# Moving the next pair's keys and queries ahead of the third gate tile in the attention stage of a hybrid encoder layer

## The chip, the cores and the metric

One NeuronCore of a Trainium2 chip runs the whole layer. The metric is device time in microseconds (us). Engines are named as in the profile: PE is TensorE (PEld its weight loads), DVE is VectorE, ACT is ScalarE, POOL is GpSimd and SP is SyncE, which here only issues DMAs.

## The reference, cut to what matters

The layer normalizes x (1024 rows, 1024 columns), projects it, runs three token mixers side by side (a short gated convolution, a strictly causal stick-breaking attention with 16 heads of 64, a cross-attention into 256 memory rows), gates and sums them, and ends with an MLP of width 4096. What this case turns on:

```
proj = rms_norm(x, g_mix) @ w_in       # conv_h|conv_B|conv_C|sb_q|sb_k|sb_v|x_q|gate_pre
for each head, each block of 128 queries:
    z = q @ k.T * 64**-0.5             # keys up to the end of the block
    log_1mb = where(past, log_sigmoid(-z), 0)
    between = reversed cumsum(log_1mb) - log_1mb
    a = where(past, exp(log_sigmoid(z) + between), 0)
    o = a @ v
gates = sigmoid(gate_pre)              # three gates of 1024 columns
x = x + (g0*y_conv + g1*y_sb + g2*y_x) @ w_out
```

## The kernel before

All matrices are float32, and each product is made of three passes with a high and a low half (`mm3`, `mm3_steps`): high by high, high by low, low by high. A weight tile of 128 columns is loaded by SP into one of four buffers (`raw`), then ACT casts the high half (L89) and DVE subtracts it from the raw value (L90) into one of three buffers (`whl`). Everything else lives in a pool of 40 pages (`pg`, 128 x 1024 float32 each), 16 of which hold the transposed and normalized x (`hT`).

The stage of the heads (L666 to L721) runs the stick-breaking attention, two heads (a pair) at a time, eight pairs. A pair has 16 steps: for each head `hd`, eight query blocks `i`. A step calls `sb_weights` (scores z on PE, L553 and L554; two sigmoids on ACT, L555 and L556; two causal masks on POOL, L558; a reversed running product on DVE, L568; a product on DVE, L572). Two steps later `sb_transpose` turns the weights on PE (L582), and ACT (L113) and DVE (L114) split them into halves; a step after that, for every second block, `sb_values` multiplies by the values on PE (L597), with the sum finished on ACT (L606), DVE (L607) and POOL (L608). Transposed blocks go through two PSUM buffers (`t`), filler projections through three (`d`).

Between these dependent pieces the loop puts independent projections, the fillers (L205 to L207). For pair p they are `gate_steps(0, p)`, `gate_steps(1, p)`, `gate_steps(2, p)`, each a column tile of one gate in 4 cuts of 12 matmuls, and `sb_qk(p+1)`: the keys (4 cuts) and then the queries (4 cuts) that the next pair needs. They are chained and handed out by a quota (`goal`, L708), 20 cuts over the 16 steps: 10 for the first head and 10 for the second. The last pair has `conv_steps(0)` in place of `sb_qk`.

What follows a projection's last matmul (`done`) is written down when the next cut is asked for. For a gate it is one sigmoid on ACT per half (L619) and, at the end, a store to DRAM issued by POOL (L621). For keys and queries it is two casts on ACT (L507, L508 or L521, L522) and two subtractions on DVE (L509, L510 or L523, L524) per half; after the keys, SP issues four DMAs that copy 64 rows to the other 64 rows (L514), and they wait for those casts and subtractions.

From L382 on nothing pins the program order (`pin[0] = False`): the order of each engine's queue is settled when the kernel is built, mostly as written, with pieces pulled ahead where something was not ready by the planner's own estimate. At run time each engine takes its queue in order.

Of the kernel before, what the change touches and what calls it, by code (L numbers as in the profile page):

```python
# [36 lines left out]
def f32v(ap):  # L37

    return ap.bitcast(F32)
# [3 lines left out]
def block_kernel(ctx, tc, x, mem, small, w_in, w_v, w_kv, w_co, w_so, w_xo, w_out, w_up, w_dn, out):  # L43
# [19 lines left out]
    def page(dt=F32R, shape=(P, 1024)):  # L63
        return pgp.tile(list(shape), dt, tag="pg", name=nm("pg"))
# [41 lines left out]
    def unit(src, paged=False):  # L106

        return halves(load(src), paged)
# [74 lines left out]
    def run(gen):  # L183
        for _ in gen:
            pass

    def chain(*gens):
        for g in gens:
            yield from g

    def fill(gen, n):
        for _ in range(n):
            next(gen, None)
# [17 lines left out]
    def project_steps(w, th, done, cuts=2):  # L211

        ps = pd()
        yield from mm3_steps(
            ps, [(cut(w, k * P, (k + 1) * P), cut(hT[k], th * 512, th * 512 + 512)) for k in range(KT)], cuts
        )
        done(ps)
# [280 lines left out]
    def sb_qk(p, st):  # L498


        ka, kb, la, lb = page(), page(), page(), page()
        w = unit(w_in[CT_K + p])
        for th in range(2):
            s = slice(th * 512, th * 512 + 512)

            def done(ps):
                nc.scalar.copy(ka[A, s], ps[A])  # L507
                nc.scalar.copy(kb[B, s], ps[B])  # L508
                nc.vector.tensor_tensor(out=la[A, s], in0=ps[A], in1=f32v(ka[A, s]), op=ALU.subtract)  # L509
                nc.vector.tensor_tensor(out=lb[B, s], in0=ps[B], in1=f32v(kb[B, s]), op=ALU.subtract)  # L510

            yield from project_steps(w, th, done)
        for t_, to, from_ in ((ka, B, A), (kb, A, B), (la, B, A), (lb, A, B)):
            nc.sync.dma_start(out=f32v(t_[to]), in_=f32v(t_[from_]))  # L514
        qa, qb = page(), page()
        w = unit(w_in[CT_Q + p])
        for th in range(2):
            s = slice(th * 512, th * 512 + 512)

            def done(ps):  # L520
                nc.scalar.copy(qa[A, s], ps[A])  # L521
                nc.scalar.copy(qb[B, s], ps[B])  # L522
                nc.vector.tensor_tensor(out=qa[B, s], in0=ps[A], in1=f32v(qa[A, s]), op=ALU.subtract)  # L523
                nc.vector.tensor_tensor(out=qb[A, s], in0=ps[B], in1=f32v(qb[B, s]), op=ALU.subtract)  # L524

            yield from project_steps(w, th, done)
        st.update(q=(qa, qb), k=(ka, kb), kl=(la, lb))

    def sb_v(p):

        raw = load(v_scr[p // 4][:, p % 4, :])
        v = []
        for jh in range(2):
            vt = page(F32R, (P, 4, 2, P))
            to = vt.rearrange("p j h e -> p (j h) e")
            src = raw[:, jh * 512 : jh * 512 + 512].rearrange("p (a e) -> p a e", a=8)
            split(src, to[:, :, 0:64], to[:, :, 64:128])
            v.append(vt)
        return v
# [3 lines left out]
    def sb_weights(st, hd, i):  # L543

        q, kh, kl = st["q"][hd], st["k"][hd], st["kl"][hd]
        W = (i + 1) * P
        be, eo = page(F32), page(F32)
        ts_ = slice(i * P, (i + 1) * P)
        for c in range(1 + (i >= 4)):
            w = W if i < 4 else W // 2  # L550
            cs = slice(w * c, w * c + w)
            z = pz()
            nc.tensor.matmul(z[:, 0:w], lhsT=q[:, ts_], rhs=kh[:, cs], start=True, stop=False)  # L553
            nc.tensor.matmul(z[:, 0:w], lhsT=q[:, ts_], rhs=kl[:, cs], start=False, stop=True)  # L554
            nc.scalar.activation(eo[:, cs], z[:, 0:w], AF.Sigmoid, scale=-0.125)  # L555
            nc.scalar.activation(be[:, cs], z[:, 0:w], AF.Sigmoid, scale=0.125)  # L556
        for t_, fill_ in ((eo, 1.0), (be, 0.0)):
            nc.gpsimd.affine_select(  # L558
                out=t_[:, W - P : W],
                in_=t_[:, W - P : W],  # L560
                pattern=[[-1, P]],
                compare_op=ALU.is_gt,
                fill=fill_,
                base=0,
                channel_multiplier=1,
            )
        rev = eo[:, W - 1 :: -1]
        nc.vector.tensor_tensor_scan(  # L568
            out=rev, data0=rev, data1=zero.broadcast_to([P, W]), initial=1.0, op0=ALU.mult, op1=ALU.add
        )  # L570

        nc.vector.tensor_tensor(out=be[:, 0 : W - 1], in0=be[:, 0 : W - 1], in1=eo[:, 1:W], op=ALU.mult)  # L572
        return be
# [38 lines left out]
    def gate_steps(b, d):  # L612
        w = unit(w_in[CT_G + 8 * b + d])
        g = page(F32)
        for th in range(2):
            yield from project_steps(
                w,
                th,
                lambda ps: nc.scalar.activation(g[:, th * 512 : th * 512 + 512], ps, AF.Sigmoid),  # L619
            )  # L620
        nc.gpsimd.dma_start(out=g_scr[b][d], in_=g)  # L621
# [3 lines left out]
    def conv_steps(c):  # L625

        prod = page(F32)
        ch = page(F32)
        w = unit(w_in[CT_H + c])
        for th in range(2):  # L630
            s = slice(th * 512, th * 512 + 512)
            yield from project_steps(w, th, lambda ps: nc.scalar.copy(ch[:, s], ps))
        w = unit(w_in[CT_C + c])
        for th in range(2):
            s = slice(th * 512, th * 512 + 512)
            yield from project_steps(
                w, th, lambda ps: nc.vector.tensor_tensor(out=prod[:, s], in0=ps, in1=ch[:, s], op=ALU.mult)
            )
        cv = page(F32)

        def tap(j):
            return sm[:, C_CONV + 3 * c + j : C_CONV + 3 * c + j + 1]

        nc.scalar.activation(cv, prod, AF.Copy, scale=tap(2))
        for j in (1, 2):
            nc.vector.scalar_tensor_tensor(
                out=cv[:, j:1024],
                in0=prod[:, 0 : 1024 - j],
                scalar=tap(2 - j),
                in1=cv[:, j:1024],  # L650
                op0=ALU.mult,
                op1=ALU.add,
            )
        w = unit(w_in[CT_B + c])
        hl = (page(), page())
        for th in range(2):
            s = slice(th * 512, th * 512 + 512)

            def done(ps):
                nc.vector.tensor_tensor(out=cv[:, s], in0=ps, in1=cv[:, s], op=ALU.mult)  # L660
                split(cv[:, s], hl[0][:, s], hl[1][:, s])

            yield from project_steps(w, th, done)
        u.append(hl)

    nxt = {}  # L666
# [9 lines left out]
    for p in range(NPAIR):  # L676
        st, nxt = nxt, {}
        st.update(p=p)
        gens = [gate_steps(b, p) for b in range(3)]
        nfill = 12  # L680
        if p + 1 < NPAIR:
            gens.append(sb_qk(p + 1, nxt))
            nfill += 8
        else:
            gens.append(conv_steps(0))
            nfill += 9
        more = chain(*gens)
        weight = [i + 4 for i in range(8)]
        total, seen, used = 2 * sum(weight), 0, 0
        for hd in range(2):  # L690
            aT = {}
            for i in range(8):
                be = sb_weights(st, hd, i)
                if hd == 0 and i == 0:
                    st["v"] = sb_v(p)

                def tail_t(st=st, hd=hd, i=i, be=be, aT=aT):
                    if "o" not in st:
                        st["o"] = page(F32)
                    if i % 2 == 0:  # L700
                        aT[i // 2] = [page(F32R, (P, 2, 2, 256)) for _ in range(i // 2 + 1)]
                    sb_transpose(be, i, aT[i // 2])

                todo.append((step[0] + 2, tail_t))
                if i % 2:
                    todo.append((step[0] + 3, lambda st=st, hd=hd, g=i // 2, aT=aT: sb_values(st, hd, g, aT.pop(g))))
                seen += weight[i]
                goal = nfill * seen // total  # L708
                half = (goal - used + 1) // 2
                fill(more, half)  # L710
                todo.sort(key=lambda e: e[0])
                flush(0)
                fill(more, goal - used - half)
                used = goal
                step[0] += 1
        if p + 1 < NPAIR:
            run(more)
# [175 lines left out]
```

## Time and profile before

| | |
|---|---|
| median of 3 runs | 2309.98 us (2309.84 to 2311.8) |
| the profiled execution | 2309.64 us, of which 2307.9 us are the profiled span |
| granted TensorE clock | 1.0 over the whole span |
| busy share of DVE, ACT, POOL | 49%, 35%, 13% |
| the stage of the heads | 332.6 to 1023.1 us of the span |
| starts of pairs 1 to 7 (first z, i = 0, of the first head) | 410.17, 495.61, 581.04, 666.47, 751.90, 837.38, 922.87 us |

A pair takes 85.43 us, and from the second pair on its timeline repeats to within some hundredths of a microsecond, so one pair can be read for all. In the timeline rows below, the columns are the start, the length, the engine, the line with operation and shape, how many neighbours are merged (x), and in brackets the idle time of the engine before it with what ended that. Matmuls overlap, so the distance from one start to the next is what one costs, not its length.

### The profile page before, as it was taken

The numbers are of one execution on the slowest core, as the hardware profiler recorded it, in microseconds if no ns is written. First come the engines' busy times: TensorE is split into PE (matmuls) and PEld (weight loads), VectorE is DVE, ScalarE is ACT, GpSimd is POOL, SyncE is SP. The second block draws the span as 40 slices with busy tenths as digits, with TensorE's granted clock in tenths as the row PEclk, the third lists the DMA queues.
The fourth block names the chain that finished last, engine by engine and source line by source line (L and its number), as shares of the span: only waits on it lengthen the run. The fifth ranks groups of instructions, "written<-read, shape, count | busy, mean of one in ns | idle before, by whom it ended". The sixth has DMA issues, their size and how long they took to land.

```text
span 2307.9 us, 26972 instructions
## 1 busy us (share of the span) xinstructions
PE 2261.2 (98%) x10688; PEld 1880.7 (81%) x10688; DVE 1130.1 (49%) x1589; ACT 803.3 (35%) x1550; POOL 303.3 (13%) x422
## 2 busy tenths in 40 slices
PE   7999999999999999999999999999999999999999
PEld 6988888778778778788888888888888888888887
DVE  5534127787777777763333344443333333333333
ACT  6544235565556555541122121223221221221221
POOL 1021113333334333320000000000000000000000
PEclk9999999999999999999999999999999999999999
DMA  6311322222122122211111443250111111111111
GB/s 220 101 60 68 125 69 76 72 75 81 64 83 73 65 90 65 83 40 52 46 47 63 146 156 128 92 191 1 37 55 55 37 55 52 40 55 48 44 46 73
DMA packets 49455, 174.79 MB, mean 76 GB/s; under 512 B 6065, under 2 KB 6065, under 8 KB 49329
## 3 DMA queue, kind: packets, MB, share of 16 engines
q1 hardware_dynamic: 42160, 147.90, 20.4%
q0 software_dynamic: 7168, 25.17, 2.9%
q8 instruction: 84, 1.38, 0.2%
q14 instruction: 43, 0.34, 0.0%
HBM read 135.29 MB, written 29.36 MB: 71 GB/s over the span
## 4 chain that ended last, share of the span: by engine, by line
PE 82%; DVE 6%; issue 5%; POOL 4%; ACT 3%; DMA 1%; SPq 0%; POOLq 0%; ACTq 0%; DVEq 0%
PE d L205 16%; PE d L207 16%; PE d L206 16%; PE d L125 9%; PE d L127 9%; PE d L126 9%; POOL pg L558 3%; PE o L597 2%; DVE pg L114 1%; PE t L582 1%; DVE pg L572 1%; ACT pg L555 1%; PE z L554 1%; PE z L553 1%; DVE pg L568 1%
## 5 line engine op out<-in xcount | busy, mean ns | idle before, releaser
L205 PE MATMUL d<-pg,whl 128*128 128x512 f32 x1664 | 655.2, 394 | 0.0
L207 PE MATMUL d<-pg,whl 128*128 128x512 f32 x1664 | 649.8, 391 | 0.0
L206 PE MATMUL d<-pg,whl 128*128 128x512 f32 x1664 | 649.4, 390 | 0.0
L207 PEld LDWEIGHTS d<-pg,whl 128*128 128x128 f32 x1664 | 312.4, 188 | 66.5
L206 PEld LDWEIGHTS d<-pg,whl 128*128 128x128 f32 x1664 | 312.7, 188 | 60.1
L205 PEld LDWEIGHTS d<-pg,whl 128*128 128x128 f32 x1664 | 312.7, 188 | 60.1
L90 DVE TENSOR_TENSOR whl<-raw,whl 128x1024 fp32r<-128x1024 f32 x160 | 201.9, 1262 | 302.3 <-ACT whl L89 301.8
L89 ACT CAST whl<-raw 128x1024 fp32r<-128x1024 f32 x160 | 168.6, 1054 | 518.4 <-PE d L127 291.5
L558 POOL TENSOR_SCALAR_AFFINE_SELECT pg<-pg 128x128 f32<-128x128 f32 x256 | 181.2, 713 | 317.4 <-ACT pg L555 301.6
L568 DVE TENSOR_TENSOR_SCAN pg<-pg,zero 128x128 f32<-128x128 f32 (+7 forms) x128 | 176.2, 1377 | 64.3 <-POOL pg L558 62.6
L127 PE MATMUL d<-whl,pg 128*128 128x512 f32 x512 | 199.2, 389 | 0.0
L125 PE MATMUL d<-whl,pg 128*128 128x512 f32 x512 | 199.2, 389 | 0.0
L126 PE MATMUL d<-whl,pg 128*128 128x512 f32 x512 | 199.2, 389 | 0.0
L113 ACT CAST pg<-t 128x256 fp32r<-128x256 f32 (+2 forms) x336 | 115.2, 364 | 212.4 <-DVE pg L114 144.7
L833 DVE TENSOR_TENSOR pg<-d,pg 128x512 f32<-128x512 f32 x128 | 88.3, 690 | 188.8 <-PE d L127 188.5
L114 DVE TENSOR_TENSOR pg<-t,pg 128x256 fp32r<-128x256 f32 (+2 forms) x336 | 129.4, 404 | 69.6 <-ACT pg L113 66.2
L126 PE MATMUL d<-pg,whl 128*128 128x512 f32 x384 | 149.4, 389 | 0.0
L125 PE MATMUL d<-pg,whl 128*128 128x512 f32 x384 | 149.4, 389 | 0.0
L127 PE MATMUL d<-pg,whl 128*128 128x512 f32 x384 | 149.4, 389 | 0.0
L205 PE MATMUL d<-pg,pg 128*128 128x512 f32 (+1 forms) x384 | 138.1, 360 | 1.3 <-ACT pg L116 1.3
L206 PE MATMUL d<-pg,pg 128*128 128x512 f32 (+1 forms) x384 | 136.9, 357 | 0.5 <-DVE pg L90 0.5
L207 PE MATMUL d<-pg,pg 128*128 128x512 f32 (+1 forms) x384 | 136.9, 357 | 0.0
(114 smaller groups left out, 2747.3 us busy)
## 6 DMA issues: line engine op xcount, KB each, us to landing
raw<-in_w_in SPq DMA_DIRECT2D x72, 512.0 KB, 3.6
raw<-in_w_up SPq DMA_DIRECT2D x32, 512.0 KB, 3.7
raw<-in_w_dn SPq DMA_DIRECT2D x32, 512.0 KB, 4.3
gscr<-pg POOLq DMA_DIRECT2D x24, 512.0 KB, 2.9
raw<-gscr SPq DMA_DIRECT2D x24, 512.0 KB, 3.3
raw<-in_w_kv SPq DMA_DIRECT2D x16, 512.0 KB, 4.4
pg<-in_x SPq DMA_DIRECT2D x16, 512.0 KB, 8.2
pg<-pg SPq DMA_DIRECT2D x32, 256.0 KB, 3.4
```

What stands on the lines that cost most here:

```text
L89: a = nc.scalar.copy(hl[0], raw)
L90: b = nc.vector.tensor_tensor(out=hl[1], in0=raw, in1=f32v(hl[0]), op=ALU.subtract)
L113: nc.scalar.copy(hi, src)
L114: nc.vector.tensor_tensor(out=lo, in0=src, in1=f32v(hi), op=ALU.subtract)
L125: nc.tensor.matmul(ps, lhsT=ah, rhs=bh, start=i == 0, stop=False)
L126: nc.tensor.matmul(ps, lhsT=ah, rhs=bl, start=False, stop=False)
L127: nc.tensor.matmul(ps, lhsT=al, rhs=bh, start=False, stop=i == n - 1)
L205: nc.tensor.matmul(ps, lhsT=ah, rhs=bh, start=i == 0, stop=False)
L206: nc.tensor.matmul(ps, lhsT=ah, rhs=bl, start=False, stop=False)
L207: nc.tensor.matmul(ps, lhsT=al, rhs=bh, start=False, stop=i == n - 1)
L558: nc.gpsimd.affine_select(out=t_[:, W - P : W], in_=t_[:, W - P : W], pattern=[[-1, P]], compare_op=ALU.is_gt, fill=fill_, base=0, channel ...
L568: nc.vector.tensor_tensor_scan(out=rev, data0=rev, data1=zero.broadcast_to([P, W]), initial=1.0, op0=ALU.mult, op1=ALU.add)
```

## The change

In the list of the fillers of a pair, `sb_qk(p + 1)` stands third, ahead of the third gate tile, and no longer last. The quota and the number of cuts are the same. The last pair's list is as before.

```
         gens = [gate_steps(b, p) for b in range(3)]
         nfill = 12
         if p + 1 < NPAIR:
-            gens.append(sb_qk(p + 1, nxt))
+            gens.insert(2, sb_qk(p + 1, nxt))
             nfill += 8
         else:
             gens.append(conv_steps(0))
```

## Rows read from the trace of the kernel before

**Rows 1.** The page, busy time of PE: us, share of the span, instructions.
```profile
PE 2261.2 (98%) x10688; PEld 1880.7 (81%) x10688; DVE 1130.1 (49%) x1589; ACT 803.3 (35%) x1550; POOL 303.3 (13%) x422
```
**Rows 2.** Busy us by engine in two stretches: length, PE, PEld, DVE, ACT, POOL.
```profile
581.00:666.40 85.40, 81.54 (x400) 67.12 (x400) 66.39 (x95) 50.18 (x117) 31.93 (x44) 1.00 0.23 74
1038.60:1096.30 57.70, 57.70 (x256) 47.80 (x255) 19.20 (x21) 11.31 (x14) 0.00 (x0) 1.00 0.17 52
```
**Rows 3.** Line L523: durations in ns (min/median/max), and who waited for it (us, times).
```profile
L523 DVE TENSOR_TENSOR pg<-d,pg x16: 683/684/685, 328.6 to 925.5; 64x512 fp32r<-64x512 f32 x16
...
  PE z L553: 7.4, 7
```
**Rows 4.** Timeline of PE where pair 4 starts.
```profile
665.05 0.39 PE L207 MATMUL d<-pg,whl 128*128 128x512 f32 x1
666.47 0.33 PE L553 MATMUL z<-pg,pg 128*128 128x128 f32 x1 [1.04 <-DVE pg L523]
...
667.65 1.95 PE L597 MATMUL o<-pg,pg 128*128 128x512 f32 x6 [0.74 <-DVE pg L114]
...
675.51 0.63 PE L582 MATMUL t<-ident,pg 128*128 128x128 f32 x4 [0.64 <-DVE pg L114]
...
679.47 1.19 PE L597 MATMUL o<-pg,pg 128*128 128x512 f32 x4 [0.78 <-DVE pg L114]
```
**Rows 5.** Timeline of PE where the second head of pair 3 starts.
```profile
624.09 0.39 PE L207 MATMUL d<-pg,whl 128*128 128x512 f32 x1
...
625.12 1.94 PE L597 MATMUL o<-pg,pg 128*128 128x512 f32 x6 [0.46 <-DVE pg L114]
...
634.61 1.87 PE L597 MATMUL o<-pg,pg 128*128 128x512 f32 x8
```
**Rows 6.** Timeline of DVE where pair 4 starts.
```profile
664.48 1.23 DVE L572 TENSOR_TENSOR pg<-pg,pg 128x1023 f32<-128x1023 f32 x1
665.73 0.68 DVE L523 TENSOR_TENSOR pg<-d,pg 64x512 fp32r<-64x512 f32 x1
666.45 0.69 DVE L524 TENSOR_TENSOR pg<-d,pg 64x512 fp32r<-64x512 f32 x1
667.17 1.29 DVE L114 TENSOR_TENSOR pg<-t,pg 128x256 fp32r<-128x256 f32 x3
669.11 0.69 DVE L523 TENSOR_TENSOR pg<-d,pg 64x512 fp32r<-64x512 f32 x1 [0.65 <-ACT pg L522]
...
670.53 0.42 DVE L568 TENSOR_TENSOR_SCAN pg<-pg,zero 128x128 f32<-128x128 f32 x1
```
**Rows 7.** Timeline of ACT where pair 4 starts.
```profile
667.63 0.37 ACT L113 CAST pg<-t 128x256 fp32r<-128x256 f32 x1 [3.84 <-DVE pg L114]
667.90 0.58 ACT L521 CAST pg<-d 64x512 fp32r<-64x512 f32 x1
...
669.10 0.28 ACT L555 ACTIVATE pg<-z 128x128 f32<-128x128 f32 x1
```
**Rows 8.** Timeline of DVE in the first steps of pair 3's second head.
```profile
632.17 0.75 DVE L114 TENSOR_TENSOR pg<-t,pg 128x256 fp32r<-128x256 f32 x2
...
633.82 0.73 DVE L114 TENSOR_TENSOR pg<-t,pg 128x256 fp32r<-128x256 f32 x2
...
636.38 1.23 DVE L90 TENSOR_TENSOR whl<-raw,whl 128x1024 fp32r<-128x1024 f32 x1 [1.36 <-ACT whl L89]
```
**Rows 9.** Timeline of ACT there: the third gate's first sigmoid.
```profile
630.71 0.62 ACT L619 ACTIVATE pg<-d 128x512 f32<-128x512 f32 x1
```
**Rows 10.** Line L621: the gates' stores issued by POOL (ns, min/median/max).
```profile
L621 POOL DMA_DIRECT2D gscr<-pg x24: 548/571/582, 347.0 to 975.2; - x24
```
**Rows 11.** Timeline of POOL where pair 4 starts.
```profile
669.44 0.54 POOL L558 TENSOR_SCALAR_AFFINE_SELECT pg<-pg 128x128 f32<-128x128 f32 x2 [5.00 <-ACT pg L555]
```
**Rows 12.** Timeline of SP in pair 3: the row copies, and the weight load behind them.
```profile
650.97 3.12 SPq L514 DMA_DIRECT2D pg<-pg  x4
658.33 0.33 SPq L83 DMA_DIRECT2D raw<-in_w_in  x1
```

More of the change, by code (lines that the diff above doesn't have):

```diff
@@ L681, in block_kernel @@
         if p + 1 < NPAIR:
-            gens.append(sb_qk(p + 1, nxt))
+            gens.insert(2, sb_qk(p + 1, nxt))
             nfill += 8
```

## The prediction

> **What bounds the kernel now.** I read the page's busy times first, then the busy times by stretch, then who waited for the queries' subtraction, and last the timelines of PE, DVE and ACT around the start of a pair. PE is busy for 2261.2 of 2307.9 us [rows 1], so PE sets the time, and only its idle time can be won by a new order of the same matmuls. Outside this stage there is next to none: in a stretch of the convolutions PE is busy for 57.70 of 57.70 us [rows 2]. In pair 3 it is busy for 81.54 of 85.40 us [rows 2], so a pair holds 3.86 us of idle PE, and seven pairs that start on queries prepared in the loop hold 27 us. That is all that can be at stake for a gain.
>
> Where in a pair it lies is read from PE's timeline. At the start of pair 4 PE idles 1.04 us before the first z, until DVE has subtracted the queries, then 0.74 us before the values (L597), then 0.64 us before a transpose and 0.78 us before the next values, the last three for a split on DVE [rows 4]: 3.20 us in the first 14 us of a pair. At the start of the second head, where the same steps run without new queries, there is one gap of 0.46 us [rows 5]. The queries' wait is found for all seven pairs: 7 times, 7.4 us [rows 3].
>
> **The change part by part.** No instruction is added or removed. The filler cuts have fixed places in the loop, and 20 of them stay 20; weight splits come every fourth cut for whichever tile is next. What moves is what follows the matmuls. Count the cuts of a pair from 0: before, cuts 8 to 11 are the third gate, 12 to 15 keys, 16 to 19 queries; after, 8 to 11 keys, 12 to 15 queries, 16 to 19 the third gate. The follow-up of a half is written with the cut after it. So at cuts 14 and 16, queries stand where keys stood, with equal work (two casts, two subtractions). At cut 18 and at the pair's end, two sigmoids stand where the queries' casts and subtractions were; at cuts 10 and 12, in the first steps of the second head, keys stand where sigmoids were. In sum two halves' work moves from the end of the pair to the start of its second head: for each half, two subtractions of 0.68 and 0.69 us [rows 6] on DVE and, on ACT, two casts of 0.58 us [rows 7] in place of one sigmoid of 0.62 us [rows 9].
>
> *Term A, the pair's start.* Before, DVE ends the last product (L572) at 665.71, then does the first half's two subtractions, and only at 667.17 the splits that the values wait for [rows 6]; the values start at 667.65, 2.60 us after the last filler matmul at 665.05 [rows 4]. After, the queries have been ready since cut 16, so z follows the filler at once, and with the two subtractions out of the queue the splits move up behind L572, to 665.73. That is 667.17 - 665.73 = 1.44 us, and the values start at about 666.21, 1.16 us after the last filler. The row that stands nearest agrees: at the second head that distance is 625.12 - 624.09 = 1.03 us [rows 5]. What is late next is thus the same split, so not all of 1.04 + 0.74 us goes. Bounds: nothing, if the splits don't move up, and 2.60 - 1.03 = 1.57 us. I take 1.44.
>
> *Term B, the two gaps after it.* Behind the values come the second half's casts and subtractions: DVE is held by them from 669.11 to about 670.50, with 0.65 us of idle before [rows 6], because ACT does its casts first, 667.90 to 669.07, and only then the sigmoid of z, 669.10 [rows 7]. After, ACT has one sigmoid there: 1.16 - 0.62 = 0.54 us less, on top of the 1.44, so z's sigmoid, its mask and the scan (L568, before at 670.53) come 1.98 us earlier; if the scan follows DVE's own queue, it is 1.44 + 1.39 = 2.83 us less what POOL's queue gives back (below), about 2.4. All that follows on DVE moves up by 2.0 to 2.4 us, PE by 1.44 alone: the splits gain 0.56 to 0.96 us on PE, and the gaps of 0.64 and 0.78 us [rows 4] shrink by so much. Bounds: nothing and 1.42. I take the middle, 0.75.
>
> *Term C, the second head.* Here the keys' work is new, and DVE has less room than its 49% say. Before, the four splits of the last block run at 632.17 (two) and 633.82 (two, to 634.55) [rows 8], and the eight values that need them start at 634.61 without a gap [rows 5]: just in time. The keys' first half takes its place at ACT's sigmoid of 630.71 [rows 9], and its 1.38 us on DVE stand ahead of the splits, which then run at about 633.6 and 635.2 to 635.95. The values' first four need only the first two splits; the fifth, (1.87 - 0.39) / 7 = 0.21 us apart, is due at 635.46 and gets its split at about 635.6. So PE loses about 0.15 us. The second half (cut 12) falls next to DVE's idle 1.36 us before L90 [rows 8], which covers it. If that cover is gone, and both halves reach PE in full, C is 2 x 1.38 = 2.76 us. Lower bound 0. I take 0.15, by the due times of the rows, which are the nearest of all.
>
> *The queues.* SP's four row copies now wait for keys that are done four cuts sooner; behind them stands a weight load that before went out at 658.33, 4.3 us after the copies ended [rows 12], so it hangs on a free buffer and not on them: nothing. POOL's store of the third gate moves from the second head's fourth step to the pair's end, ahead of the first masks. POOL is held there for its wait and 0.57 us [rows 10], and the masks, which before came after 5.00 us of idle [rows 11], would start 0.6 us later than they could: this is in B's lower value. The subtractions themselves cost the same anywhere, 683 to 685 ns in 16 cases [rows 3].
>
> *Pages.* Counted from the code in program order, from first write to last read, the stage needs at most 36 of 40 pages before and 38 after, because keys and queries are held longer. The Trainium skill (Perfetto Trace Analysis, Optimization Strategy) says that the same gap repeating on the engine that should be saturated can mean that there is not enough buffer space for the next tile. The gaps here do repeat every 85.43 us, yet the rows name a subtraction and splits as what ended them, so I don't follow it; by it the change, which holds more pages, would give nothing back and lose time, and that is the third rival.
>
> **The sum.** A + B - C = 1.44 + 0.75 - 0.15 = 2.04 us a pair. Seven pairs have B and A at their start, and seven have C: 7 x 2.04 = 14.3 us. The profiled execution took 2309.64 us, so 2295.4; the median of the runs is 0.34 higher, so I predict 2295.7 us. The mechanism's own range: with all of both gaps, 7 x (1.44 + 1.42) = 20.0 less, 2290.0; with A alone and C at 0.9 us, 7 x 0.54 = 3.8 less, 2306.2.
>
> **The rivals.** (1) *The wait is handed on.* The z no longer waits, but the splits keep their place (the planner of the queues may put a weight split of 1.23 us [rows 8] or the product of the last block ahead of them), and the values start when they did: A and B nothing, about 2310. For it: three of the four gaps already name L114 and not the queries. Against it: nothing but the subtractions stood between L572 and the splits. (2) *The second head becomes the tight place.* The keys' 2.76 us hit the values and transposes of the second head in full, and the first head gains A alone: 7 x (1.44 - 2.76) = 9.2 us slower, 2319.2. It decides from C above A + B, that is with more than 2.2 us of the 2.76 uncovered. For it: splits that end 0.06 us before they are due. Against it: the same steps before have 1.36 us of idle DVE behind them. (3) *Pages run out*, and a step's sigmoids must wait until the next values free a page. That costs a pair about one cut of 12 matmuls, 12 x 57.70 / 256 = 2.70 us [rows 2], against the 2.04 won: 7 x 0.66 = 4.6 us slower, 2314.6. For it: two pages of slack instead of four, and any piece that is pulled ahead takes two. Against it: no row shows a wait for a page.
>
> **How the numbers follow.** The forecast has 0.66 (2290 to 2301), the same mechanism with C eating most of B or more (2301 to 2305.4) 0.13, the wait handed on 0.11, the second head 0.06, pages 0.04. A measurement of this kernel tells 0.2%, 4.6 us, from no change. Faster by more than that is 0.66 + 0.13 = 0.79; within it, the first rival and half of the third, 0.13; slower, the second and the rest, 0.08. The range is 2289.5 to 2305.5: it takes in the bounds of A and B from the fast side and leaves out the rivals, some 0.2.
>
> **What would show it right or wrong.** Right: at the start of each pair no gap before z, values 1.1 to 1.3 us after the last filler in place of 2.60, pairs of 83.2 to 83.8 us in place of 85.43, and DVE's keys at the second head's first steps with a gap of less than 0.5 us on PE. Step A is wrong if values still start 2.6 us after the filler; B if the gaps of 0.64 and 0.78 us stay; C if PE idles over 1 us before the values some 10 us into the second head. A sigmoid that waits for a page would mean rival 3. The whole is wrong if the pairs are no shorter than 84.8 us.

## The result, and the profile after

The changed kernel takes 2297.67 us in the median of 4 runs (2297.51 to 2298.66), the kernel before 2310.43 (4 runs): a ratio of 0.9945, 95% interval 0.9928 to 0.9962, or 12.8 us less. Predicted were 2295.7, within 2289.5 to 2305.5. The profiled execution took 2298.66 us, the slowest of the four, so 11.0 us less than the profiled one of before. The granted clock averaged 1.0 of full speed (2.4 GHz) in all four executions of the changed kernel and 0.994 to 1.0 in 70 further ones of the kernel before, of which the 16 at 1.0 took 2309.74 us in the median, so that at full clock the gain is 12.1 us.

The page after, and the busy times (length, PE, PEld, DVE, ACT, POOL) of pair 3:

```profile
PE 2261.7 (98%) x10688; PEld 1882.5 (82%) x10688; DVE 1127.5 (49%) x1589; ACT 801.7 (35%) x1550; POOL 298.2 (13%) x422
```
```profile
577.60:661.40 83.80, 81.46 (x401) 67.23 (x401) 66.11 (x96) 49.83 (x117) 30.93 (x44) 1.00 0.25 76
```

PE is as busy as before [rows 1, 2]; what went away is idle time: 83.80 - 81.46 = 2.34 us in a pair in place of 3.86. The pairs 1 to 6 took 502.84 us in place of 512.70, 1.64 us less each. Behind the stage nothing changed: from its last values to the end it is 1284.9 us in both traces.

The timeline of PE where pair 4 starts, after:

```profile
661.20 0.39 PE L207 MATMUL d<-pg,whl 128*128 128x512 f32 x1
661.42 0.22 PE L553 MATMUL z<-pg,pg 128*128 128x128 f32 x1
...
662.42 1.94 PE L597 MATMUL o<-pg,pg 128*128 128x512 f32 x6 [0.66 <-DVE pg L114]
...
669.17 0.63 PE L582 MATMUL t<-ident,pg 128*128 128x128 f32 x4 [0.71 <-DVE pg L114]
...
672.84 2.10 PE L597 MATMUL o<-pg,pg 128*128 128x512 f32 x8
```

Against [rows 4]: z follows the filler with no gap, the values start 1.22 us after the last filler in place of 2.60, the gap before the transpose stays (0.71 us for 0.64), and the one before the next values is gone.

PE's order is not the same in this stretch, though. The planner that settles the queues put five fillers that ran between z and the transposes behind them, and the eight values, which stood as two, four and two, in one piece. Before, these rows stand between those of [rows 4]:

```profile
673.55 0.40 PE L205 MATMUL d<-pg,whl 128*128 128x512 f32 x1
...
674.48 0.39 PE L206 MATMUL d<-pg,whl 128*128 128x512 f32 x1
...
678.08 0.61 PE L597 MATMUL o<-pg,pg 128*128 128x512 f32 x2
```

From 17 us behind the last filler to the end of the pair the two orders agree again, and there PE starts out 2.2 us ahead. DVE at the pair's start, where the queries' subtractions of [rows 6] are no more and the three splits come right behind the product:

```profile
660.80 1.23 DVE L572 TENSOR_TENSOR pg<-pg,pg 128x1023 f32<-128x1023 f32 x1
661.95 1.28 DVE L114 TENSOR_TENSOR pg<-t,pg 128x256 fp32r<-128x256 f32 x3
664.15 1.39 DVE L114 TENSOR_TENSOR pg<-raw,pg 128x512 fp32r<-128x512 f32 x2 [0.92 <-ACT pg L113]
665.46 0.50 DVE L568 TENSOR_TENSOR_SCAN pg<-pg,zero 128x128 f32<-128x128 f32 x1
```

At the second head of pair 3 PE shows the other side (the first row is from before, the others from after). The first values wait 0.38 us as before (0.46), but the eight values of the last block, which ran through in [rows 5], now break after two, and take 632.51 - 630.16 = 2.35 us to the next transpose in place of 636.32 - 634.61 = 1.71 before:

```profile
636.32 0.27 PE L582 MATMUL t<-ident,pg 128*128 128x128 f32 x1
```
```profile
620.66 1.95 PE L597 MATMUL o<-pg,pg 128*128 128x512 f32 x6 [0.38 <-DVE pg L114]
...
630.16 0.61 PE L597 MATMUL o<-pg,pg 128*128 128x512 f32 x2
631.12 1.54 PE L597 MATMUL o<-pg,pg 128*128 128x512 f32 x6 [0.35 <-DVE pg L114]
632.51 0.27 PE L582 MATMUL t<-ident,pg 128*128 128x128 f32 x1
```

DVE there has the keys' first half ahead of the four splits of [rows 8], and no idle time is left before L90, where it was 1.36 us:

```profile
627.72 0.68 DVE L509 TENSOR_TENSOR pg<-d,pg 64x512 fp32r<-64x512 f32 x1
628.41 0.69 DVE L510 TENSOR_TENSOR pg<-d,pg 64x512 fp32r<-64x512 f32 x1
629.14 0.76 DVE L114 TENSOR_TENSOR pg<-t,pg 128x256 fp32r<-128x256 f32 x2
...
630.67 0.73 DVE L114 TENSOR_TENSOR pg<-t,pg 128x256 fp32r<-128x256 f32 x2
...
633.22 1.23 DVE L90 TENSOR_TENSOR whl<-raw,whl 128x1024 fp32r<-128x1024 f32 x1
```

### The profile page after: what moved, and what is told of

It reads as the page before. It is cut to its first block, busy times and chain, and to the rows that moved or that the text cites. A ratio compares the mean times of both kernels' runs of the same rounds, so it can differ in the third digit from the quotient of the medians.

```text
span 2297.0 us, 26957 instructions
## 1 busy us (share of the span) xinstructions
PE 2261.7 (98%) x10688; PEld 1882.5 (82%) x10688; DVE 1127.5 (49%) x1589; ACT 801.7 (35%) x1550; POOL 298.2 (13%) x422
## 4 chain that ended last, share of the span: by engine, by line
PE 85%; DVE 5%; issue 3%; ACT 3%; POOL 3%; DMA 1%; SPq 0%; POOLq 0%; ACTq 0%; DVEq 0%
PE d L207 17%; PE d L206 17%; PE d L205 17%; PE d L125 9%; PE d L126 9%; PE d L127 9%; POOL pg L558 2%; PE o L597 2%; DVE pg L114 1%; PE t L582 1%; DVE pg L572 1%; PE z L554 1%; PE z L553 1%; DVE whl L90 1%; ACT pg L555 1%
## 5 line engine op out<-in xcount | busy, mean ns | idle before, releaser
L90 DVE TENSOR_TENSOR whl<-raw,whl 128x1024 fp32r<-128x1024 f32 x160 | 200.0, 1250 | 293.4 <-ACT whl L89 292.6
L558 POOL TENSOR_SCALAR_AFFINE_SELECT pg<-pg 128x128 f32<-128x128 f32 x256 | 167.9, 662 | 304.8 <-ACT pg L555 293.9
L114 DVE TENSOR_TENSOR pg<-t,pg 128x256 fp32r<-128x256 f32 (+2 forms) x336 | 129.3, 404 | 65.5 <-ACT pg L113 62.0
```

The costliest lines, as they stand in the source:

```text
L90: b = nc.vector.tensor_tensor(out=hl[1], in0=raw, in1=f32v(hl[0]), op=ALU.subtract)
L114: nc.vector.tensor_tensor(out=lo, in0=src, in1=f32v(hi), op=ALU.subtract)
L558: nc.gpsimd.affine_select(out=t_[:, W - P : W], in_=t_[:, W - P : W], pattern=[[-1, P]], compare_op=ALU.is_gt, fill=fill_, base=0, channel ...
```

## The experiments

Twelve kernels. Theory throughout: what counts is where the follow-up work of keys and queries stands in DVE's queue, measured against the splits (L114) that PE's transposes and values wait for. In kernels with added lines the profile's line numbers are one to eleven higher than in the listing. Ratios are to the kernel before, run beside each set of kernels. Its median moved by 0.75 us between the sets (2309.68 to 2310.43), and the changed kernel stands as measured above, so differences from the changed kernel of about 1 us say nothing. The edits are shown cut to what matters.

**The first half of the keys, later.** The casts and subtractions of the keys' first half are written with cut 11 in place of 10:

```
-            yield from project_steps(w, th, done)
+            for _ in project_steps(w, th, later):   # later: pend.append((done, ps))
+                yield
+                while pend:
+                    f, got = pend.pop(0)
+                    f(got)
```

> The changed kernel, with the casts and subtractions of the keys' first half written one cut later (cut 11 in place of 10), behind the last block's splits. Theory (place in DVE's queue): the 0.61 us a pair that the second head loses goes, 7 x 0.61 = 4.3 us less than the changed kernel, 2293.4. Rival (the keys' work in the second head costs wherever it stands): within 1 us of 2297.7.

Measured: 2295.46 us, ratio 0.9934 (0.9921 to 0.9946), about 2.2 us less than the changed kernel. The break in the eight values is gone (1.70 us to the next transpose) while PE's order is that of the changed kernel, so the place in DVE's queue is what made it. But only half of it reaches the time: at the pair's start the values now come 576.32 - 574.88 = 1.44 us after the last filler, 0.22 later than in the changed kernel. PE, let through earlier, meets DVE later on.

```profile
576.32 0.73 PE L608 MATMUL o<-pg,pg 128*128 128x512 f32 x2 [0.88 <-DVE pg L114]
```
```profile
627.90 1.87 PE L608 MATMUL o<-pg,pg 128*128 128x512 f32 x8
629.60 0.27 PE L593 MATMUL t<-ident,pg 128*128 128x128 f32 x1
```

**The keys' subtractions doubled**, in the changed kernel, for the first half (cut 10) or the second (cut 12):

```
+                for _ in range(2 if th == 0 else 1):      # or th == 1
                     nc.vector.tensor_tensor(out=la[A, s], ...)
                     nc.vector.tensor_tensor(out=lb[B, s], ...)
```

> The changed kernel, with the two subtractions of the keys' first half (cut 10) written twice. Theory (the loss at the second head comes from what stands in DVE's queue ahead of the last block's splits): 7 x 1.37 = 9.6 us more than the changed kernel's 2297.7, so 2307. Rival (the loss comes from ACT, two casts of 0.58 us in place of a sigmoid of 0.62 us, while DVE has room): within 2 us of 2297.7.

> The changed kernel, with the two subtractions of the keys' second half (cut 12) written twice, the same 1.37 us of DVE a pair two cuts later. Theory (only the place ahead of the splits costs; here DVE had 1.36 us of idle time before the change): under 2 us more than the changed kernel's 2297.7. Rival (the second head has no room on DVE at all, the sum of the load counts): as much as the first half doubled, some 9.6 us, 2307.

Measured: 2308.31 us for the first half (0.999, 0.9981 to 0.9999), some 10.6 us more than the changed kernel, near the theory's 9.6; 2303.8 for the second (0.9972, 0.9962 to 0.9983), 6.1 more, between the two forecasts. With the first half doubled, the build also moved a z and fillers between the eight values, so part of its number may be that; with the second doubled, PE's order is that of the changed kernel. So the first half's place looks the dearer, DVE has no room at either, and there is not the room at cut 12 that I read from the 1.36 us of idle time [rows 8]: the first half's work had already filled it. In pair 3 the second half's extra work comes out 18 us later, as one gap before values that had none:

```profile
654.97 0.62 PE L598 MATMUL o<-pg,pg 128*128 128x512 f32 x2 [0.31 <-DVE pg L114]
```

**The queries' first half doubled**, in the kernel before, the same edit at L523 and L524:

> The kernel before, with the two subtractions of the queries' first half (cut 18) written twice, so 1.37 us more on DVE at that place and nothing else new. Theory (they stand in DVE's queue ahead of the splits that the values wait for, and every microsecond there is PE's): 7 x 1.37 = 9.6 us slower than before, 2320; the first values start about 4.0 us after the last filler in place of 2.6. Rival (the wait for the queries is only handed on, the splits set the start of the values on their own): within 2 us of 2310.

Measured: 2311.02 us, ratio 0.9998 (0.9989 to 1.0007). The theory missed; the rival's number fits, but the run decides neither. The wait before z did grow from 1.04 to 2.53 us, but the build put the next z and a filler matmul ahead of the values, and the later gaps shrank, so this is not the same queue with more work in it:

```profile
584.02 0.30 PE L554 MATMUL z<-pg,pg 128*128 128x128 f32 x1 [2.53 <-issue]
...
585.15 0.73 PE L598 MATMUL o<-pg,pg 128*128 128x512 f32 x2 [0.20 <-DVE pg L114]
```

**One subtraction doubled**, in the kernel before: the one that z waits for (L523) or the one behind it (L524), both of the first half. PE's order is untouched in both, DVE's is not:

```
-                nc.vector.tensor_tensor(out=qa[B, s], ...)
+                for _ in range(2 if th == 0 else 1): nc.vector.tensor_tensor(out=qa[B, s], ...)
```

> The kernel before, with only the first subtraction of the queries' first half (L523) written twice, PE's order the same as before. Theory (splits in DVE's queue) and rival (wait before z) both say 0.68 us a pair: 4.8 us slower than before, 2314.9. A third theory (what is lost before z is won back behind it, because the values wait for something else anyway): within 1 us of 2310.1.

> The kernel before, with only the second subtraction of the queries' first half (L524) written twice: 0.69 us more on DVE behind the one that z waits for and ahead of the splits; PE's order is the same as before. Theory (the splits in DVE's queue set when the values start, and so what the pair's start costs): z still waits 1.04 us, the values start 0.69 us later, 7 x 0.69 = 4.8 us slower than before, 2314.9. Rival (the wait for the queries before z is what costs): no change, within 1 us of 2310.1.

Measured: 2310.42 us (1.0002, 0.9993 to 1.0011) and 2310.22 us (1.0004, 0.9996 to 1.0013): no cost in either. The theory's number missed again; for the first the third theory's fits, for the second the rival's. But in both the build put one of the three splits ahead of the extra subtraction, so the first split is not late by all of it: the values start 2.89 us after the last filler in the first kernel, and at 2.60, as before, in the second, where they then break after two. In the first, PE waits for z until 2.64 us after the last filler in place of 1.42. Some eleven microseconds after the last filler PE is within 0.05 us of before in both. DVE tells why, in the first:

```profile
580.51 0.68 DVE L523 TENSOR_TENSOR pg<-d,pg 64x512 fp32r<-64x512 f32 x1
581.23 0.42 DVE L114 TENSOR_TENSOR pg<-t,pg 128x256 fp32r<-128x256 f32 x1
581.69 0.68 DVE L523 TENSOR_TENSOR pg<-d,pg 64x512 fp32r<-64x512 f32 x1
582.40 0.69 DVE L524 TENSOR_TENSOR pg<-d,pg 64x512 fp32r<-64x512 f32 x1
583.12 0.76 DVE L114 TENSOR_TENSOR pg<-t,pg 128x256 fp32r<-128x256 f32 x2
583.91 0.68 DVE L523 TENSOR_TENSOR pg<-d,pg 64x512 fp32r<-64x512 f32 x1
```

The second half's subtraction had 0.65 us of idle time before it [rows 6]; here it has none, and it starts 583.91 - 579.83 = 4.08 us after the last filler, where it did at 4.06 (669.11 - 665.05). In the second kernel it starts 4.08 us after the last filler too. The extra work went into that idle time, and PE's lost time was won back in the gaps that follow.

**The last subtraction doubled**, in the kernel before (L524 of the second half), behind that idle time:

> The kernel before, with only the last subtraction of the queries' second half (L524) written twice: 0.69 us more on DVE behind its idle 0.65 us at the pair's start, where the same extra work ahead of that idle time cost nothing. Theory (DVE's queue, with its idle time, sets when PE gets past the first 14 us of a pair): 7 x 0.69 = 4.8 us slower than before, 2314.7. Rival (some other chain, through ACT or POOL, sets it, and DVE has room): within 1.5 us of 2309.8.

Measured: 2310.17 us (1.0002, 0.9993 to 1.0011). A miss too. DVE does run 0.87 us late 14 us into the pair, but here the build put fillers and a z between the values, PE passes that stretch 0.2 us later than before, and the pair ends 0.07 us later:

```profile
595.26 0.72 PE L597 MATMUL o<-pg,pg 128*128 128x512 f32 x2
595.82 0.39 PE L553 MATMUL z<-pg,pg 128*128 128x512 f32 x1
...
596.88 1.21 PE L597 MATMUL o<-pg,pg 128*128 128x512 f32 x4 [0.21 <-DVE pg L114]
```

**Keys early, queries where the change put them** (first gate, keys, second gate, queries, third gate; `sb_qk` is split into `sb_k` and `sb_q`):

```
-            gens.insert(2, sb_qk(p + 1, nxt))
+            gens = [gens[0], sb_k(p + 1, nxt), gens[1], sb_q(p + 1, nxt), gens[2]]
```

> Keys and queries as two fillers: first gate, keys, second gate, queries, third gate. The keys' work then falls to cuts 6 and 8 (first head, steps 6 and 7), the queries' stays at cuts 14 and 16 as in the changed kernel, and cuts 10 and 12 at the second head's start carry sigmoids again. Theory (place on DVE: the second head's start is tight, the first head's late steps are not): the changed kernel's loss of 0.61 us a pair goes and nothing else moves, 7 x 0.61 = 4.3 us less, 2293.4. Rival (all of a pair's steps are equally tight on DVE, or keys held longer run out of pages): 2297.7 or more.

Measured: 2310.58 us (1.0003, 0.9994 to 1.0012): the whole gain is lost, and the theory's picture of the first head was wrong. The keys' work in steps 6 and 7 of the first head does to the second head what the queries' work did to the next pair. The pair's start is as in the changed kernel (values 1.27 us after the last filler in pair 3), and the eight values no longer break, but the second head's first values wait 2.02 us:

```profile
625.49 0.22 PE L557 MATMUL z<-pg,pg 128*128 128x128 f32 x1
...
627.84 0.73 PE L601 MATMUL o<-pg,pg 128*128 128x512 f32 x2 [2.02 <-DVE pg L114]
628.41 0.60 PE L586 MATMUL t<-ident,pg 128*128 128x128 f32 x4
629.64 1.08 PE L601 MATMUL o<-pg,pg 128*128 128x512 f32 x4 [0.63 <-DVE pg L114]
```

This z waits for nothing, since its queries have long been there: the late splits alone set the start of the values. On DVE the subtractions of the keys' second half stand around the last product, ahead of these splits:

```profile
624.83 0.66 DVE L509 TENSOR_TENSOR pg<-d,pg 64x512 fp32r<-64x512 f32 x1
625.41 1.21 DVE L576 TENSOR_TENSOR pg<-pg,pg 128x1023 f32<-128x1023 f32 x1
626.64 0.69 DVE L510 TENSOR_TENSOR pg<-d,pg 64x512 fp32r<-64x512 f32 x1
627.36 0.76 DVE L114 TENSOR_TENSOR pg<-t,pg 128x256 fp32r<-128x256 f32 x2
```

Here, and in the next kernel, the build also put four transposes between the second and the third of these values, which in the changed kernel run in one piece; the gap of 0.63 us stands in that new order.

**Keys and queries first:**

```
-            gens.insert(2, sb_qk(p + 1, nxt))
+            gens.insert(0, sb_qk(p + 1, nxt))
```

> Keys and queries are the first filler, ahead of all three gates, so their work falls to cuts 2, 4, 6 and 8, all in the first head, and the pages are held longest: 40 of 40 at the peak by the same count as 36 before and 38 in the changed kernel. Theory (place on DVE): the second head is free of it, the first head's later steps pay some: between 2293 and 2298. Rival (pages bound it: the more are held, the slower): slower than the changed kernel by at least the 4.6 us that the third rival gave, 2302 or more.

Measured: 2310.99 us (1.0006, 0.9997 to 1.0015). The theory's range missed; the rival's number fits, but not its cause. One part of the loss is again the wait for splits at the second head:

```profile
629.79 0.73 PE L597 MATMUL o<-pg,pg 128*128 128x512 f32 x2 [2.28 <-DVE pg L114]
```

At the pair's start, behind a second head without any such work, the values start 0.40 us after the last filler, the shortest of all. Pair 3 so takes 84.55 us, 0.78 more than in the changed kernel; over seven pairs that would be 5.5 us (an estimate), of the 12.0 us between the profiled executions.

The other part goes with the clock. In six stretches of this trace, 23.9 us together, the granted clock is half of full speed, 1.2 GHz in place of 2.4; each begins within 1.8 us of the end of that wait at a second head, in which PE had idled for 1.9 to 2.8 us. A filler matmul then comes every 0.43 us in place of 0.23:

```profile
546.91 0.63 PE L205 MATMUL d<-pg,whl 128*128 128x512 f32 x1
547.34 0.63 PE L206 MATMUL d<-pg,whl 128*128 128x512 f32 x1
...
550.55 0.40 PE L205 MATMUL d<-pg,whl 128*128 128x512 f32 x1
550.78 0.39 PE L206 MATMUL d<-pg,whl 128*128 128x512 f32 x1
```

The pairs 1, 2, 4, 5 and 6, each with one such stretch, take 85.03 to 87.06 us, 5.3 us more in all than five times pair 3. All eleven executions of this kernel have a mean clock of 0.994 or 0.995. Why the clock falls stays open: pair 3 has the same wait and no fall. With the keys early it matters little: the three executions at full clock took 2308.5 to 2308.9 us.

**Fewer pages**, in the changed kernel:

```
-N_PAGES = 40
+N_PAGES = 38
```

> The changed kernel with a pool of 38 pages in place of 40, which is its own count at the peak of the stage of the heads, so no page is to spare there. Theory (queues, not pages): within 2 us of 2297.7, and pairs of 83.8 us. Rival (pages bound the stage): pairs longer by 0.66 us or more, 4.6 us or more in all, 2302.

Measured: 2299.3 us (0.9953, 0.9937 to 0.9969). Pair 3 takes 83.68 us (83.77 in the changed kernel), with as much idle time:

```profile
576.90:660.50 83.60, 81.37 (x401) 67.20 (x400) 66.00 (x96) 49.77 (x117) 30.95 (x44) 1.00 0.25 76
```

In the traces the stage is 0.8 us shorter than in the changed kernel, and what follows it is longer (1286.6 us from its last values to the end in place of 1284.9). So with none to spare pages don't bound the stage; with keys and queries first none is to spare either, and its trace names splits and the clock.

**Keys first, queries apart; and all four halves in steps 3 and 4.** In the second kernel the queries stand between the two halves of the second gate:

```
+            gens = [sb_k(p + 1, nxt), gens[0], gens[1], sb_q(p + 1, nxt), gens[2]]
# and:
+            gens = [sb_k(p + 1, nxt), gens[0], *gate_around(1, p, sb_q(p + 1, nxt)), gens[2]]
```

> Order of the fillers: keys, first gate, second gate, queries, third gate; PE's order is that of the changed kernel. The keys' work falls to cuts 2 and 4 (first head, steps 3 and 4), away from the last two steps of both heads and from the second head's first steps. Theory (work on DVE costs only in the last two steps of a head and the first two of the next): the second head's loss of 0.61 us a pair goes and its first values wait no longer than in the changed kernel: 2291 to 2294. Rival (any of this work costs wherever it stands in the first head): 2297.7 or more.

> As the kernel with keys first and queries apart, but the queries two cuts earlier, between the two halves of the second gate, so that all four halves' work falls to steps 3 and 4 of a head (cuts 2, 4, 12, 14); PE's order is that of the changed kernel. Theory (the last two steps of a head must be free on DVE): besides the second head's 0.61 us, the values at a pair's start wait less too, 0.2 to 0.8 us a pair: 2288 to 2292. Rival (the steps 3 and 4 have as little room): 2294 or more.

Measured: 2293.54 us (0.993, 0.9917 to 0.9943) and 2288.91 us (0.9909, 0.9895 to 0.9923), both as forecast; the second is 8.8 us under the changed kernel and the fastest of all. PE's order is the same in both and in the changed kernel, so these two differ in the place of the queries' work on DVE and ACT and in what moves along with it (a sigmoid and some weight splits): after the last filler the first values of pair 3 come 0.62 us earlier, and the pair is 0.65 us shorter. PE of the second at the start of pair 3 (573.37: z; the last filler at 573.14) and at the second head:

```profile
573.37 0.22 PE L557 MATMUL z<-pg,pg 128*128 128x128 f32 x1
...
573.67 1.95 PE L601 MATMUL o<-pg,pg 128*128 128x512 f32 x6
```
```profile
615.55 1.95 PE L601 MATMUL o<-pg,pg 128*128 128x512 f32 x6 [0.26 <-DVE pg L114]
...
625.08 1.87 PE L601 MATMUL o<-pg,pg 128*128 128x512 f32 x8
626.78 0.27 PE L586 MATMUL t<-ident,pg 128*128 128x128 f32 x1
```

All orders side by side, pair 3, from PE's timelines (us; first values counted from the last filler, the eight values from their start to the transpose behind them). The granted clock is 1.0 in pair 3 of every trace:

| order | cuts of the four halves' work | first values, pair | first values, second head | eight values, second head | pair |
|---|---|---|---|---|---|
| before | 14, 16, 18, end | 2.61 | 1.02 | 1.71 | 85.43 |
| changed | 10, 12, 14, 16 | 1.21 | 0.94 | 2.34 | 83.77 |
| keys' first half later | 11, 12, 14, 16 | 1.44 | 0.98 | 1.71 | 83.49 |
| keys early | 6, 8, 14, 16 | 1.27 | 2.59 | 1.71 | 85.37 |
| keys and queries first | 2, 4, 6, 8 | 0.40 | 2.84 | 1.70 | 84.55 (at half clock in part: to 87.06) |
| keys first, queries apart | 2, 4, 14, 16 | 1.14 | 0.84 | 1.71 | 83.02 |
| all in steps 3 and 4 | 2, 4, 12, 14 | 0.52 | 0.82 | 1.71 | 82.37 |

## Why the prediction was right

The time, the sign and the main mechanism, the queries' work on DVE ahead of the splits, were right. Term C was mis-sized, and term B fits in size, but beside a change of PE's order that the prediction did not foresee. The gain was 12.8 us (12.1 at full clock, 11.0 between the profiled executions) for 14.3. By its steps, against pair 3 or the mean of pairs 2 to 6:

- **Bound.** Right: PE's busy time is unchanged, and 3.86 us of idle time a pair became 2.34.
- **Term A**, predicted 1.44: 1.40. The splits moved up behind L572, the waits 1.04 and 0.74 became one of 0.66, as foreseen with the same split late next. That the place on DVE sets the start of the values with PE's order unchanged is shown by the last two kernels.
- **Term B**, predicted 0.75: about 0.8. Twenty microseconds into a pair PE is 2.2 us ahead of before, A included. I left open which gap would shrink: the second went whole, the first stayed. But I reckoned with PE's old order, and the planner changed it in just this stretch; no run takes the queries' work away with the old order kept, so how much of the 0.8 us is DVE's earlier splits is not shown, and that the size fits may be luck.
- **Term C**, predicted 0.15: 0.6, the term that was mis-sized. I had the splits at the right distance but gave the third of them to the fifth value. But PE stops after two values, and the third, due at 630.16 + 2 x 0.23 = 630.62 (0.23 us apart, not 0.21: only the last of the eight is narrower), starts at 631.12, right behind the third split, which begins at 630.67 and ends at 631.07. So it is the third value that needs the third split. Seven times 0.45 us are 3.2 us, about the gap between 14.3 and the 11.0 of the profiled executions; between the medians it is 1.5. That the place is the cause is shown by the later first half, whose eight values run through. That only half of it comes back in time, and that doubling the second half costs 6.1 us, shows that the second head has less room on DVE than "1.36 us of idle time covers the second half" took for granted.
- **Queues and pages.** Nothing of SP or POOL ended a wait of PE at these places. The Trainium skill's rule of the repeating gap (Perfetto Trace Analysis, Optimization Strategy) pointed to buffer space; with two pages fewer the pairs are as long, so here it did not hold for the pages.
- **Rivals.** The wait was not handed on in this kernel, but two of the other orders do just that, to the other head. The second head did become tighter, by 0.6 and not by 2.76 us.

What the runs corrected is the reading of A and B as prices. Taking the queries' work away won 2.2 us a pair; putting 0.68 to 1.37 us more about the same place cost nothing, since an idle time on DVE behind it, later gaps of PE and, where the build changed an order, other work took it up. None of these four kernels kept both queues as they were, so they don't show what a microsecond in the same queue costs. Where PE's order did stay, between the last two kernels, 0.62 us at the pair's start was 0.65 us of the pair. Why PE's pair comes out at 85.4 to 85.5 us with 0, 0.68 or 0.69 us of it added, in three different builds, is explained for two of them by the idle 0.65 us, which both use up; for the third, with the last subtraction doubled, it stays partly open.

## What to carry to other kernels

When fillers are woven into a dependent chain, look not at the filler's own matmuls but at the step where its follow-up work lands on the vector engine: it belongs where that engine has just finished the long steps' backlog, here steps 3 and 4 of a head, and not in the last two steps, whose splits the next head's first values wait for. Before pricing a wait, look for idle time further down the same queue: here 0.65 us of it took up 0.68 us of extra work at no cost, and a gain ahead of it can be smaller than the wait. Read from the trace which of several like instructions a consumer waits for; they need not stand in the order of the code. And compare the order of the queues, and the granted clock, before and after each edit: work added or moved can change both, and then the time is not the price of the work alone.
